# Moving block re-joins, a block sum, low parts and early weight sums from VectorE to GpSimd around two seven-product stages

## The chip, the cores and the metric

The kernel runs on one core of a Trainium2 chip. The core has a matrix engine (TensorE, PE in the profile), VectorE (DVE), ScalarE (ACT), GpSimd (POOL) and SyncE (SP, which here issues DMAs). Each engine works through its own list of instructions in order, and semaphores tie the lists together. The metric is the time of one execution in microseconds (us), the median over runs.

## The reference, cut to what matters

One transformer block over 1024 tokens of width 1024, with a context of 256 tokens. The part the change touches is two large projections in 32-bit floats:

```python
h_lat = _modulate(_rmsnorm(x, norm1_g), sh1, sc1)
u, v, q, k, vv, r, af, ab, ga, gb = split(h_lat @ w_in)     # w_in 1024 x 7200
b_lat = _gla_out(gated_linear_attention(q, k, vv, af, ab), r)   # 4 heads
a_lat = _chunk_mlp(u, v)
x = x + g1 * ((sigmoid(ga) * (a_lat @ w_branch_a) + sigmoid(gb) * (b_lat @ w_branch_b)) @ w_out)
h2 = _modulate(_rmsnorm(x, norm2_g), sh2, sc2)
a, g = split(h2 @ w_ffn_in)                                  # w_ffn_in 1024 x 5632
x = x + g2 * ((silu(g) * a) @ w_ffn_out)
return _rmsnorm(x, final_norm_g)
```

## The kernel before

A float32 product is made of three matrix passes: each operand is split into a high part (a rounded copy, made by ScalarE) and a low part (the operand less its high part, made by VectorE), and the passes are high by high, high by low and low by high. The split of a moving operand is `parts_of` (ScalarE L637, VectorE L638); that of a weight is `split_w` (ScalarE L236, VectorE L237).

The columns gb, u, r and ga of `w_in` (the "h stage", 16 column pairs in `todo`, 4 each) and all of `w_ffn_in` (the "FFN stage", 44 column blocks of 128 in 22 pairs) are multiplied by a scheme of seven block products instead of eight. The activations are four blocks B11, B12, B21, B22 (half of the 1024 inputs by 512 tokens) and the weights of a pair four blocks A11 to A22. The combinations are, for the activations, T3 = B22 − B12, T2 = T3 + B11, T1 = B12 − B11, T4 = B21 − T2, and for the weights S3 = A11 − A21, S2 = A22 − S3, S1 = S2 + A11, S4 = A12 − S2. The seven products are A11·B11, A12·B21, S3·T3, S2·T2, S1·T1, A22·T4 and S4·B22. One product is 12 matmuls of 128x512 (4 slices of the inputs by 3 passes). One pair is called a quad. The block raws and their parts are kept as two tiles of 128x1024 each, so that a combination of blocks is two vector instructions of 128x1024, and the low part two more. The weight sums S3, S2 (VectorE L700, L701) and S1, S4 (L702, L703) are four instructions of 128x512 per quad, followed by two low parts of 128x1024 (L638) and that of A22 (L710).

Ahead of a stage, when the activations' second half is not ready yet, the first quads do A11·B11 and A12·B21 alone (`early_quads`, six quads in the h stage, four in the FFN stage). `run_quads` then walks the pairs: for these early quads it does the other five products (`others`), for the later ones all seven. In `weights_s` the engine of S1 and S4 is an argument: GpSimd for the later quads, VectorE for the early ones.

`others` is the order around the change: S3·T3 into bank X, ScalarE copies X to q7 (L736), S2·T2 adds to X, VectorE makes u3 (L741), GpSimd q7 = u3 − q7 (L742), S1·T1 into bank Y, u3 += Y (L744), A22·T4 into X, p1 += X (L747), S4·B22 into Y, q7 += Y (L750). The five products of an early quad are 60 matmuls, a later quad's seven are 84.

The h stage sits behind the gated linear attention, a loop over four heads. A head's function calls `between`, which for heads 0 to 2 makes the gates of the next head, and for the last (head 3) emits four early quads of the h stage and `h_first`: B22 and B12 re-joined from their high and low parts (`h_raw`, L871), T3 = B22 − B12 in place (L877) and T3's parts. The rest of head 3 is scores (matmuls L565, masked copies L569, their sum att L573), outputs (matmuls L582, L583, L586), the norm's factor (rstd: VectorE L171, GpSimd L172, ScalarE L596), and a transpose back (PE L605, VectorE L610). After the loop come two more early quads and `h_others`: B11 re-joined, T1 over B12, T2 over B11, T1 and T2 split, B21 re-joined, T4 over B21. Early in head 3 the loop also makes two modulation vectors: VectorE multiplies and adds rows of `w_ada` (L930), PE spreads them (L934) and VectorE takes the diagonal (L936, L937).

In the FFN stage the blocks come raw from a transpose (`block_T`), and `other_operands` makes T3, T2, the first quad's weight sums (the callback `after`), T1, T4 and B22's parts, all combinations and low parts on VectorE.

The order on every engine but PE is set by a scheduler from the order in which the program is written and from when operands become ready; PE's order in these parts is that in which the matmuls are written. Tiles come from pools: 40 buffers of 128x1024 (`slot`), three raw weight tiles in flight, and eight banks of PSUM.

Of the kernel before, what the change touches and what calls it, by code (L numbers as in the profile page):

```python
# [17 lines left out]
P = 128  # L18
# [15 lines left out]
def block_kernel(  # L34
# [598 lines left out]

    def parts_of(raw, shape=(P, 2, 512)):

        hi, lo = slot(list(shape), F32R), slot(list(shape), F32R)
        nc.scalar.copy(hi, raw)  # L637
        nc.vector.tensor_sub(lo, raw, f(hi))  # L638
        return hi, lo
# [9 lines left out]

    def moving(tiles):  # L650
        return [parts_of(t) for t in tiles]

# [17 lines left out]
    def other_operands(op, blk, after):  # L670

        b11, b21, b12, b22 = blk[0][0], blk[1][0], blk[0][1], blk[1][1]
        dve = (nc.vector, nc.vector)
        t3 = combined("tensor_sub", b22, b12, dve)
        op["T3"] = moving(t3)
        t2 = combined("tensor_add", t3, b11, dve)
        op["T2"] = moving(t2)
        after()
        op["T1"] = moving(combined("tensor_sub", b12, b11, dve))
        op["T4"] = moving(combined("tensor_sub", b21, t2, dve))  # L680
        op["B22"] = moving(b22)

# [81 lines left out]
    def run_quads(op, todo, quads, hook=None):  # L764

        for fi, (w, cols, sink) in enumerate(todo):
            if fi < len(quads):
                if fi:
                    weights_s(*weights(w, cols), quads[fi]["ops"], nc.vector)
                others(quads[fi], op, sink)  # L770
# [95 lines left out]

    def h_raw(j, t):
        out = []
        for hi, lo in h_moving(j, t):
            o = slot([P, 2, 512])  # L870
            nc.vector.tensor_add(o, f(hi), f(lo))  # L871
            out.append(o)
        return out
# [10 lines left out]

    def h_others(op, b22, b12, after):
        b11 = h_raw(0, 0)
        in_place("tensor_sub", b12, b12, b11)
        in_place("tensor_add", b11, b11, b22)
        op["T2"] = moving(b11)
        after()  # L890
        op["T1"] = moving(b12)
        b21 = h_raw(1, 0)
        in_place("tensor_sub", b21, b21, b11)
        op["T4"] = moving(b21)
# [70 lines left out]
    for h in range(HEADS):  # L965
        now, ahead = ahead, None

        def between():
            if h + 1 < HEADS:
                global_next.append(head_gates(h + 1))  # L970
                return
            p1s.extend(four())
            for at in range(0, 4, 2):
                quads.extend(early_quads(h_op, todo, at, bank, p1s[at:at + 2]))
            sums.extend(h_first(h_op))
            global_next.append(None)
# [432 lines left out]
```

## Time and profile before

| | us |
|---|---|
| three runs | 1767.29, 1767.95, 1770.74 (median 1767.95) |
| profiled execution | 1771.97 |
| its span | 1770.2 |
| TensorE's mean granted clock in it | 0.993 of full speed |
| busy: PE, DVE, ACT, POOL | 1712.4 (97%), 1138.8 (64%), 668.5 (38%), 215.4 (12%) |

The busy rows say that PE is the engine that has work nearly always. The 3% in which it has none are spread over the span, and two slices of the profile's 40 are worse: PE shows 8 tenths at the start, and the clock row shows 8 tenths in slice 27 (1150 to 1195 us). The page gives each engine's mean over the whole span. What holds PE in a stretch is seen in the timeline of that stretch, where each row has a start, a time, the instruction with its count, and in brackets the idle time before it with the engine and tile whose event ended it.

### The profile page before, as it was taken

How to read it: one execution, taken by the hardware profiler on the slowest of the kernel's cores; microseconds unless marked ns; L12 is line 12 of the kernel's file. 1: busy time of each engine (PE TensorE's matmuls, PEld its weight loads, DVE VectorE, ACT ScalarE, POOL GpSimd, SP SyncE). 2: the span in 40 equal slices, each digit the busy share in tenths (PEclk: the TensorE clock that was granted, in tenths of full speed). 3: DMA queues.
4: the chain of work that ended last, by engine and by line, in shares of the span. 5: the costliest groups of instructions: out<-in, count | busy, mean ns of one | idle time of the engine just before them, and what ended most of it. 6: DMA issues, size and time to landing. Idle time of an engine off the chain costs nothing.

```text
span 1770.2 us, 21603 instructions
## 1 busy us (share of the span) xinstructions
PE 1712.4 (97%) x8162; PEld 1407.5 (80%) x8162; DVE 1138.8 (64%) x1559; ACT 668.5 (38%) x974; POOL 215.4 (12%) x193
## 2 busy tenths in 40 slices
PE   8899999999899999999999999989999999999997
PEld 3887888888678888877888888768888888888886
DVE  7686595867865464277656745885545555466797
ACT  6663423323443434234322213533333333355343
POOL 2220000000112353000000000012122122000001
PEclk9999999999999999999999999989999999999999
DMA  9511234052354454387858951233222232377572
GB/s 339 156 37 36 85 118 179 24 179 60 113 155 133 129 179 125 124 293 260 262 190 308 321 191 74 70 116 98 77 90 83 75 92 84 127 242 277 180 270 99
DMA packets 219961, 267.89 MB, mean 151 GB/s; under 512 B 11920, under 2 KB 142032, under 8 KB 219856
## 3 DMA queue, kind: packets, MB, share of 16 engines
q1 hardware_dynamic: 219040, 265.08, 45.1%
q0 software_dynamic: 720, 1.40, 0.2%
q8 instruction: 64, 1.05, 0.2%
q14 instruction: 41, 0.34, 0.1%
q10 hardware_dynamic: 96, 0.02, 0.0%
HBM read 205.64 MB, written 60.82 MB: 151 GB/s over the span
## 4 chain that ended last, share of the span: by engine, by line
PE 79%; DVE 11%; DMA 4%; issue 3%; ACT 3%; POOL 1%; SPq 0%; DVEq 0%; ACTq 0%; POOLq 0%
PE m L716 20%; PE g L716 17%; PE m L273 13%; PE m L1283 5%; PE g L1283 5%; PE m L1166 5%; PE m L285 4%; PE g L538 2%; DVE s L638 1%; PE m L822 1%; DVE wlo L237 1%; DVE s L422 1%; PE g L822 1%; DMA s<-in_w_ada_dram 1%; PE g L1363 1%
## 5 line engine op out<-in xcount | busy, mean ns | idle before, releaser
L716 PE MATMUL m<-s,s 128*128 128x512 f32 x1320 | 313.5, 395 | 8.8 <-ACT q L736 3.8
L716 PEld LDWEIGHTS m<-s,s 128*128 128x128 f32 x1320 | 251.0, 191 | 65.1 <-ACT q L736 5.8
L273 PE MATMUL m<-s,whi 128*128 128x512 f32 (+1 forms) x832 | 252.3, 384 | 2.2 <-ACT s L990 1.5
L237 DVE TENSOR_TENSOR wlo<-wr,whi 128x1024 fp32r<-128x1024 f32 x92 | 112.4, 1224 | 194.2 <-ACT whi L236 194.0
L716 PE MATMUL g<-s,s 128*128 128x512 f32 x960 | 225.0, 391 | 9.0 <-ACT q L736 4.1
L716 PEld LDWEIGHTS g<-s,s 128*128 128x128 f32 x960 | 179.2, 188 | 51.6 <-ACT q L736 6.6
L273 PEld LDWEIGHTS m<-s,whi 128*128 128x128 f32 x832 | 154.0, 188 | 33.2 <-ACT s L990 2.4
L236 ACT CAST whi<-wr 128x1024 fp32r<-128x1024 f32 x92 | 96.5, 1051 | 214.1 <-PE m L273 107.9
L273 PE MATMUL m<-s,wlo 128*128 128x512 f32 (+1 forms) x416 | 158.9, 383 | 1.8 <-DVE wlo L237 1.8
L637 ACT CAST s<-s 128x1024 fp32r<-128x1024 f32 x98 | 102.4, 1052 | 134.4 <-DVE s L638 62.2
L638 DVE TENSOR_TENSOR s<-s,s 128x1024 fp32r<-128x1024 f32 x98 | 145.4, 1494 | 9.9 <-ACT s L637 6.0
L172 POOL TENSOR_TENSOR rstd<-rstd,nhalf 128x1 f32<-128x1 f32 (+2 forms) x43 | 29.1, 678 | 847.7 <-DVE rstd L171 847.6
L285 PE MATMUL m<-whi,s 128*128 128x256 f32 x640 | 126.0, 291 | 0.1
L716 PE MATMUL g<-s,whi 128*128 128x512 f32 x384 | 118.5, 390 | 0.0
L638 DVE TENSOR_TENSOR s<-wr,s 128x1024 fp32r<-128x1024 f32 x77 | 92.3, 1233 | 22.8 <-ACT s L637 22.1
L285 PEld LDWEIGHTS m<-whi,s 128*128 128x128 f32 x640 | 101.5, 192 | 4.2 <-issue 2.7
L742 POOL TENSOR_TENSOR q<-u,q 128x512 f32<-128x512 f32 x38 | 59.4, 1563 | 314.1 <-DVE u L741 150.3
L637 ACT CAST s<-wr 128x1024 fp32r<-128x1024 f32 x77 | 78.2, 1053 | 49.9 <-DMA wr<-wsT 25.3
L285 PE MATMUL m<-wlo,s 128*128 128x256 f32 x320 | 92.3, 289 | 2.6 <-DVE wlo L237 1.9
L273 PEld LDWEIGHTS m<-s,wlo 128*128 128x128 f32 x416 | 78.3, 188 | 16.6 <-DVE wlo L237 2.0
L1166 PE MATMUL m<-s,s 128*128 128x512 f32 x384 | 87.6, 390 | 0.0
L1166 PEld LDWEIGHTS m<-s,s 128*128 128x128 f32 x384 | 72.0, 188 | 14.9
(293 smaller groups left out, 2879.2 us busy)
## 6 DMA issues: line engine op xcount, KB each, us to landing
wr<-in_w_in_dram SPq DMA_DIRECT2D x82, 512.0 KB
s<-in_w_ada_dram SPq DMA_DIRECT2D x48, 512.0 KB
wr<-in_w_ffn_in_dram SPq DMA_DIRECT2D x48, 512.0 KB
wr<-actd SPq DMA_DIRECT2D x77, 256.0 KB
s<-in_w_ffn_out_dram SPq DMA_DIRECT2D x22, 512.0 KB
wsT<-s SPq DMA_DIRECT2D x44, 256.0 KB
wr<-wsT SPq DMA_DIRECT2D x44, 256.0 KB
wr<-in_w_ffn_out_dram SPq DMA_DIRECT2D x33, 256.0 KB
```

The lines of the kernel that those rows point to most:

```text
L236: nc.scalar.copy(hi, raw)
L237: lo_sub[0] = nc.vector.tensor_sub(lo, raw, f(hi)).ins
L273: nc.tensor.matmul(ps, ws[a][:, k, :], get(b, k, t0, n), start=k == 0 and i == 0, stop=k == nk - 1 and i == 2)
L285: nc.tensor.matmul(ps[:, j, :], get(b, 4 * kh + k, (2 * tp + j) * P, P), ws[a][:, k, :], start=kh == 0 and j == 0 and k == 0 and i == 0, s ...
L538: r = nc.tensor.matmul(pkv[:, j, :], kt[:, j, :], vt(n), start=j == 0, stop=True, skip_group_check=True)
L637: nc.scalar.copy(hi, raw)
L638: nc.vector.tensor_sub(lo, raw, f(hi))
L716: pe(nc.tensor.matmul(ps, wts[a][:, k, :], mov[k // 2][b][:, k % 2, :], start=start and k == 0 and i == 0, stop=k == 3 and i == 2, skip_gr ...
L742: nc.gpsimd.tensor_sub(q7, u3, q7)
L822: pe(nc.tensor.matmul(banks[tt], op[mov][kp][b][:, kk, tt * P:(tt + 1) * P], wts[a][:, kk, :], start=start and kp == 0 and kk == 0 and i = ...
L1166: pe(nc.tensor.matmul(ps, yF.get(b, k, tt * P, P), wo[k // 2][a][:, k % 2, :], start=k == 0 and i == 0, stop=k == KT - 1 and i == 2))
L1283: pe(nc.tensor.matmul(banks[tt], o[b][:, 0, tt * P:(tt + 1) * P], o[a][:, 1, :], start=start and k == 0 and i == 0, stop=k == KH - 1 and i ...
```

## The change

In the h stage, B11 and B21 are re-joined on GpSimd (4 instructions of 128x1024) and the code that does it stands in `between` of the last head, ahead of the early quads, and no longer after the loop. T2 is made in place over T3's raw (B22's buffer) and T1 from B12 as before, T4 = B21 − T2.

In the FFN stage, T1 is computed on GpSimd right after T3, and the low parts of B22 are made on GpSimd ahead of `after`, where they stood last on VectorE.

In `run_quads`, S1 and S4 of the early quads but the first are added on GpSimd, which are five quads in the h stage and three in the FFN stage. The instruction counts are 1512 to 1488 on VectorE and 194 to 218 on GpSimd. ScalarE's and SyncE's do not change, and PE's list is the same, row by row. Below line 638 the line numbers are one higher than before, below 884 one lower.

```diff
-    def parts_of(raw, shape=(P, 2, 512)):
+    def parts_of(raw, shape=(P, 2, 512), eng=nc.vector):
...
-        nc.vector.tensor_sub(lo, raw, f(hi))
+        eng.tensor_sub(lo, raw, f(hi))
...
-    def moving(tiles):
-        return [parts_of(t) for t in tiles]
+    def moving(tiles, eng=nc.vector):
+        return [parts_of(t, eng=eng) for t in tiles]
...
-        dve = (nc.vector, nc.vector)
-        t3 = combined("tensor_sub", b22, b12, dve)
+        both = nc.vector, nc.vector
+        t3 = combined("tensor_sub", b22, b12, both)
+        t1 = combined("tensor_sub", b12, b11, (nc.gpsimd, nc.gpsimd))
         op["T3"] = moving(t3)
-        t2 = combined("tensor_add", t3, b11, dve)
+        t2 = combined("tensor_add", t3, b11, both)
         op["T2"] = moving(t2)
+        op["B22"] = moving(b22, nc.gpsimd)
         after()
-        op["T1"] = moving(combined("tensor_sub", b12, b11, dve))
-        op["T4"] = moving(combined("tensor_sub", b21, t2, dve))
-        op["B22"] = moving(b22)
+        op["T1"] = moving(t1)
+        op["T4"] = moving(combined("tensor_sub", b21, t2, both))
...
-                    weights_s(*weights(w, cols), quads[fi]["ops"], nc.vector)
+                    weights_s(*weights(w, cols), quads[fi]["ops"], nc.gpsimd)
...
-    def h_raw(j, t):
+    def h_raw(j, t, eng=nc.vector):
...
-            nc.vector.tensor_add(o, f(hi), f(lo))
+            eng.tensor_add(o, f(hi), f(lo))
...
-    def h_others(op, b22, b12, after):
-        b11 = h_raw(0, 0)
+    def h_others(op, b22, b12, b11, b21, after):
+        in_place("tensor_add", b22, b22, b11)
+        op["T2"] = moving(b22)
+        after()
         in_place("tensor_sub", b12, b12, b11)
-        in_place("tensor_add", b11, b11, b22)
-        op["T2"] = moving(b11)
-        after()
         op["T1"] = moving(b12)
-        b21 = h_raw(1, 0)
-        in_place("tensor_sub", b21, b21, b11)
+        in_place("tensor_sub", b21, b21, b22)
         op["T4"] = moving(b21)
...
+            raws = h_raw(0, 0, nc.gpsimd), h_raw(1, 0, nc.gpsimd)
             p1s.extend(four())
...
-            sums.extend(h_first(h_op))
+            sums.extend(h_first(h_op) + raws)
```

On VectorE in the tail of head 3, the rows before the change are the masked copies, the two sums att and the norm's factor (`rstd`, from the sums of squares `ss`), with the low part L638 of the h stage's T3 ahead of them:

```order
L638 TENSOR_TENSOR s_3964<-s_3951,s_3963 128x1024
L569 COPY_PREDICATED s_127<-mask_lo,g_3975 128x512
L573 TENSOR_TENSOR att_3981<-s_127 128x512
L569 COPY_PREDICATED s_127<-mask_up,g_3983 128x512
L569 COPY_PREDICATED s_127<-mask_lo,g_3989 128x512
L573 TENSOR_TENSOR att_3995<-s_127 128x512
L171 TENSOR_SCALAR rstd_4008<-ss_754_4005 128x2
L610 TENSOR_SCALAR s_3967<-g_4029,pcol 128x256
```

The same place after the change, where L878 is the in-place sum or difference (s_3957 and s_3959 are T2's tiles, s_3961 and s_3963 T1's, s_3819 and s_3821 the re-joined B11):

```order
L638 TENSOR_TENSOR s_3972<-s_3959,s_3971 128x1024
L569 COPY_PREDICATED s_127<-mask_lo,g_3983 128x512
L878 TENSOR_TENSOR s_3957<-s_3957,s_3819 128x1024
L573 TENSOR_TENSOR att_3989<-s_127 128x512
L878 TENSOR_TENSOR s_3959<-s_3959,s_3821 128x1024
L569 COPY_PREDICATED s_127<-mask_up,g_3991 128x512
L569 COPY_PREDICATED s_127<-mask_lo,g_3997 128x512
L878 TENSOR_TENSOR s_3961<-s_3961,s_3819 128x1024
L573 TENSOR_TENSOR att_4003<-s_127 128x512
L878 TENSOR_TENSOR s_3963<-s_3963,s_3821 128x1024
L171 TENSOR_SCALAR rstd_4016<-ss_758_4013 128x2
```

Four sums of 128x1024 have moved up from behind the head to between the masked copies and the factor.

On GpSimd, the rows of the same part after the change are the DMA of a row for the modulation, the four re-joins (L872), and the powers for the norm's factor (L172); before, the powers followed the DMA directly:

```order
L925 DMA s_3674<-in_b_ada_dram 1x16x64
L872 TENSOR_TENSOR s_3819<-s_921,s_925 128x1024
L872 TENSOR_TENSOR s_3821<-s_922,s_926 128x1024
L872 TENSOR_TENSOR s_3823<-s_923,s_927 128x1024
L872 TENSOR_TENSOR s_3825<-s_924,s_928 128x1024
L172 TENSOR_TENSOR rstd_4016<-rstd_4016,nhalf 128x2
```

The first of them takes a buffer that an ada row's product (L930 before, L929 after) held last.

On GpSimd at the start of the FFN stage after the change stand the norm's power, T1's two differences (L646), B22's two low parts (L638), the first quad's q7 (L743), and the weight sums of the second quad (L703, L704); before, q7 followed the norm's power directly:

```order
L172 TENSOR_TENSOR rstd_8958<-rstd_8958,nhalf 128x1
L646 TENSOR_TENSOR s_9183<-s_9037,s_8823 128x1024
L646 TENSOR_TENSOR s_9185<-s_9038,s_8824 128x1024
L638 TENSOR_TENSOR s_9208<-s_9039,s_9207 128x1024
L638 TENSOR_TENSOR s_9212<-s_9040,s_9211 128x1024
L743 TENSOR_TENSOR q_1595_9258<-u_1596_9259,q_1595_9258 128x512
L703 TENSOR_TENSOR s_9337<-s_9336,wr_9332 128x512
L704 TENSOR_TENSOR s_9337<-wr_9332,s_9336 128x512
```

Four instructions of 128x1024 are new ahead of the first q7, and two of 128x512 behind it.

## Rows read from the trace of the kernel before

**Rows 1.** Windows of 25 us: length, busy time of each engine (instructions), clock, DMA share, GB/s

```profile
450.00:475.00 25.00, 20.50 (x84) 15.15 (x83) 23.71 (x26) 13.21 (x15) 3.25 (x1) 1.00 0.23 63
1125.00:1150.00 25.00, 21.05 (x89) 16.11 (x88) 24.72 (x25) 13.57 (x15) 2.15 (x1) 1.00 0.28 83
1150.00:1175.00 25.00, 21.47 (x67) 16.49 (x68) 19.74 (x27) 9.58 (x13) 1.61 (x1) 0.73 0.36 107
```

**Rows 2.** Timeline of PE, h stage: start, us, instruction, [idle before <-releaser]

```profile
458.15 0.73 PE L716 MATMUL g<-s,s 128*128 128x512 f32 x2 [2.06 <-ACT s L637]
462.83 5.76 PE L716 MATMUL g<-s,s 128*128 128x512 f32 x24 [0.73 <-ACT q L736]
...
495.63 13.91 PE L716 MATMUL g<-s,s 128*128 128x512 f32 x60 [0.68 <-ACT q L736]
510.22 13.90 PE L716 MATMUL g<-s,s 128*128 128x512 f32 x60 [0.68 <-ACT q L736]
```

**Rows 3.** Timeline of PE, start of the FFN stage

```profile
1134.12 2.88 PE L716 MATMUL m<-s,s 128*128 128x512 f32 x12
1138.75 5.96 PE L716 MATMUL m<-s,s 128*128 128x512 f32 x25 [1.75 <-ACT q L736]
...
1150.16 5.04 PE L716 MATMUL m<-s,s 128*128 128x512 f32 x14 [1.55 <-DVE u L744]
1157.85 4.63 PE L716 MATMUL m<-s,s 128*128 128x512 f32 x10 [2.65 <-DVE s L638]
1163.20 15.87 PE L716 MATMUL m<-s,s 128*128 128x512 f32 x60 [0.72 <-ACT q L736]
1179.75 14.12 PE L716 MATMUL m<-s,s 128*128 128x512 f32 x60 [0.68 <-ACT q L736]
1194.55 5.74 PE L716 MATMUL m<-s,s 128*128 128x512 f32 x24 [0.68 <-ACT q L736]
```

**Rows 4.** Groups of POOL by form: line, op, shapes, count | busy, mean ns | idle before

```profile
L702 POOL TENSOR_TENSOR s<-s,wr 128x512 f32<-128x512 f32 x28 | 36.0, 1287 | 221.2 <-DVE s L701 146.9 <-PE g L716 30.7 <-issue 27.3
L196 POOL TENSOR_TENSOR s<-raw,s 128x256 fp32r<-128x256 f32 x4 | 3.1, 783 | 9.2 <-DVE raw L195 9.2
```

**Rows 5.** Timeline of DVE, head 3, early part

```profile
372.40 1.23 DVE L237 TENSOR_TENSOR wlo<-wr,whi 128x1024 fp32r<-128x1024 f32 x1 [0.18 <-ACT whi L236]
373.55 3.79 DVE L930 SCALAR_TENSOR_TENSOR s<-s,cs,s 128x1024 f32<-128x1024 f32 x3
...
393.23 1.29 DVE L483 SCALAR_TENSOR_TENSOR s<-m,s 128x512 f32<-128x512 f32 x2 [3.03 <-PE m L273]
394.44 1.28 DVE L936 TENSOR_TENSOR adat<-g,ident 128x512 f32<-128x512 f32 x2
```

**Rows 6.** Timeline of POOL, h stage

```profile
468.88 3.25 POOL L742 TENSOR_TENSOR q<-u,q 128x512 f32<-128x512 f32 x1 [24.93 <-DVE u L741]
499.91 1.60 POOL L742 TENSOR_TENSOR q<-u,q 128x512 f32<-128x512 f32 x1 [12.50 <-DVE u L741]
```

**Rows 7.** Timeline of DVE, beside those of POOL

```profile
468.62 2.35 DVE L638 TENSOR_TENSOR s<-s,s 128x1024 fp32r<-128x1024 f32 x2
...
500.40 1.66 DVE L702 TENSOR_TENSOR s<-s,wr 128x512 f32<-128x512 f32 x1
```

**Rows 8.** Timeline of DVE, head 3, tail

```profile
433.96 0.17 DVE L171 TENSOR_SCALAR rstd<-ss 128x2 f32<-128x2 f32 x1
...
448.72 4.62 DVE L877 TENSOR_TENSOR s<-s,s 128x1024 f32<-128x1024 f32 x4
```

**Rows 9.** Timeline of PE, head 3, tail

```profile
435.49 0.91 PE L605 MATMUL g<-ident,on 128*128 128x128 f32 x4
```

**Rows 10.** Timeline of DVE, start of the FFN stage

```profile
1132.96 2.43 DVE L638 TENSOR_TENSOR s<-s,s 128x1024 fp32r<-128x1024 f32 x2
```

**Rows 11.** Windows of 4 us of PE: length, busy (instructions), clock, DMA share, GB/s

```profile
36.00:40.00 4.00, 4.00 (x21) 0.50 1.03 411
56.00:60.00 4.00, 1.40 (x11) 1.00 0.02 4
```

## The prediction

> **What bounds the kernel now.** I read the page first: PE is busy for nearly the whole span, so a change on other engines is worth what it takes from PE's idle time, or from the time that PE runs at the lower of its two clock levels. Then windows of 25 us, to find where PE is idle [rows 1]: at the start of both stages that the change touches it works about 21 of 25 us, and there VectorE is busy 23.7 and 24.7 of 25, while GpSimd does 3.3 and 2.2. From 1150 us the mean granted clock is 0.73. So at these two places VectorE is the bound and GpSimd is free, and the question is what it takes to use that.
>
> The timeline of PE gives the sizes. In the h stage S3·T3 starts after 2.06 us of idle time [rows 2], on a ScalarE cast of VectorE's work. The five products of a quad take 13.9 us and a wait of 0.68 stands between two quads, so a quad that waits for nothing takes 510.22 − 495.63 = 14.59. From the first S2·T2 (462.83) to the third (495.63) are 32.80 us, two quads of 14.59 are 29.18: 3.6 us are lost. With the 2.06 ahead there are 5.7 to win. In the FFN stage from the first S2·T2 (1138.75) to the fourth (1194.55) are 55.80 us [rows 3], three quads are 43.77: 12.0 are lost. A part of that is clock: the 24 matmuls at 1150.16 and 1157.85 take 9.67 where 24 at 13.91/60 would be 5.56, so 4.1, and the quad at 1163.20 takes 15.87 for 13.91, so 1.96 more. Together a fall of the clock was worth 6.1 here, and 5.9 were waits.
>
> **The h stage.** Four costs and gains.
>
> The re-joins on GpSimd. No row of 128x1024 on GpSimd exists. 128x512 is 1.29 us and 128x256 is 0.78 [rows 4], so 0.51 per 256 columns, and 128x1024 about 1.29 + 2 × 0.51 = 2.3; I call it an estimate. They start when the first ada products free their buffers, near 372 us, and so run beside the chain of VectorE's multiply-adds [rows 5]. Does one engine hold up the other? The trace has it both ways: GpSimd's q7 at 499.91 ran to 501.51, and VectorE's L702 issued at 500.40 took 1.66 where it otherwise takes 0.69, ending 0.55 after it; but GpSimd's q7 at 468.88, issued just after two low parts of VectorE, took 3.25, and VectorE's two took 2.35 as ever [rows 6, 7]. The one issued second waits. All of these are two-tensor operations; no row has the multiply-add beside GpSimd. If it is held like them: four spells of 2.3 less the 0.14 that overlap (0.69 − 0.55), so 2.2 each, 8.8 us; VectorE was idle 0.18 and 3.03 in this stretch [rows 5], which takes 3.2 off, and the diagonal at 394.44, for which PE waits with its next banks, is late by 5.6. If it isn't held: 0. Between them I take two thirds, 3.7, since four instructions queued back to back on each side will alternate, and VectorE is then the second more often than not. Both ends stay for the range.
>
> The Trainium skill's page "SBUF — State Buffer", section "Who interferes with whom", says that "A DVE instruction with two SBUF inputs contends with a GpSimd instruction that reads SBUF", and that issue order decides which one blocks. The two meetings above agree with it (1.66 for 0.69). By the rule the multiply-add, which has two tensor inputs, would be held too, this term would be 5.6 and my sum 1.9 higher; no row here shows that form.
>
> The sums in the tail. In the built order four sums of 128x1024 stand between the masked copies and the norm's factor of head 3. Behind that factor on VectorE are queued the other factors and the scalings L610; for it wait GpSimd's power, ScalarE's scaling, and PE's transpose at 435.49, which had no time to spare [rows 9]. A sum is 4.62 / 4 = 1.16 us [rows 8], four are 4.6; about 0.3 of it falls in VectorE's gaps between these copies, so the factor goes from 433.96 to 438.3 and PE is late by 4.3. I see no way in which this costs nothing: the order is fixed and the sums have all their inputs by then. If the re-joins are late themselves, it is more.
>
> What is won behind it. From VectorE at the start of the stage go the four re-joins and the two thirds of the in-place work that have now been done, 6 × 1.16 = 6.9 us behind 445, four of them the 4.62 [rows 8]. T2's low parts are then ready when the early quads end, the 2.06 goes, and the T1 and T4 work, which held the first two quads, is ahead of PE. I count the whole of the loss as won: early quads ended at 458.15 − 2.06 = 456.1 [rows 2] and now end at 456.1 + 3.7 + 4.3 = 464.1, S3·T3 takes 2.8, the wait 0.68, so S2·T2 starts at 467.6, the third one 29.18 later at 496.7. Before it was 495.63 [rows 2]: +1.1.
>
> The weight sums of five early quads on GpSimd take 2 × 1.29 us instead of 2 × 0.69 each. A quad is 14.59 us and the low parts of the sums are wanted only near its end for the next one, so I count nothing; were that cover gone, it would be 1.2 a quad, and a held VectorE up to 1.2 more, as in the row at 500.40. This goes for the FFN's three quads as well.
>
> So the h stage gives +1.1, with +3.0 and −2.6 as its ends (5.6 and 0 for the 3.7).
>
> **The FFN stage.** T1's two differences and B22's two low parts go to GpSimd, 4 × 1.16 = 4.6 us off VectorE, and q1's sums another 1.4. But they are early: T1 runs beside T3's split, B22's low parts beside the first quad's weight sums, with VectorE full [rows 1]. What these four hold VectorE up is again between 0 and 4 × 2.2 = 8.8; two thirds are 5.9. For S3's low part PE waits: it came at 1132.96 + 1.2 = 1134.1, and S3·T3 started at once [rows 3, 10]. So S3·T3 moves to 1134.1 + 5.9 = 1140.0, S2·T2 to 1140.0 + 2.9 + 0.68 = 1143.6, 4.8 later than now. From there VectorE has only T1's split and T4 before A22·T4, six instructions of 1.16 with the sums' second low part and A22's (1.2 and 0.7), 8.9 us for the 9 that PE needs until then; the quads run free, and the fourth S2·T2 stands at 1143.6 + 43.77 = 1187.4, where it was 1194.55: −7.2. That keeps the clock up throughout. If nothing is held, all 12.0 are won.
>
> **The clock.** The idle time is now in two larger pieces: in the tail of head 3 PE has a wait of over 4 us, and from the early quads' end, near 1135, to 1140 nearly nothing. Did such pieces lower the clock before? Both answers are in the rows: from 1150 to 1175, where the 24 matmuls stand between waits, the mean is 0.73 [rows 1, 3], and at 36 us a busy PE has 0.50; yet at 56 to 60 us, with PE busy 1.40 of 4, it is 1.00 [rows 11]. I take one short fall at each place, at the price of the quad at 1163.20, 1.96 each: 3.9.
>
> **Sum.** 1.1 − 7.2 + 3.9 = −2.2 on 1771.97 for the profiled execution: 1769.8. This execution was 4.0 above the median of the runs, 1767.95, and the change is taken off that: 1765.7.
>
> **The rivals.**
>
> *Clearly faster.* GpSimd is the one that gives way, as at 468.88 [rows 6], or the clock doesn't fall. With the 3.7 and 5.9 held but no fall it is 1.1 − 7.2 = −6.1, 1761.8; with nothing held and no fall −2.6 − 12.0 = −14.6, 1753.3. The middle is 1757. For it: four of GpSimd's instructions are issued in the open, and one can begin only behind VectorE's running one. Against: VectorE's list is full there, so that it meets all of them.
>
> *Slower.* Place: the two idle pieces above. Mechanism: the fall of the clock is whole, as it was at 1150, not short. Price: 6.1 each instead of 1.96, −6.1 + 12.2 = +6.1: 1774.0. It decides where PE does less than it did between 1147 and 1160 before, when the clock fell. For it: 1137 to 1140 would have no matmul at all. Against: the 1.00 at 56 to 60.
>
> *No effect on either.* What the h stage loses in the tail it wins at the quads, and in the FFN stage PE waits for something that doesn't move (raw weights from DMA, three tiles in flight, or ScalarE's casts, whose B22 parts now stand ahead of S3's): 1768, within a few tenths per cent.
>
> **How the numbers follow.** About 3.5 us, 0.2%, is what a measurement of this kernel can tell from no change. My forecast 0.40; clearly faster 0.27; slower 0.21; no effect 0.12. The forecast's own range is 1761 to 1770, a fall more or fewer on either side, and lies partly below 1764.4: of its 0.40 I count 0.14 as faster, 0.22 as the same, 0.04 as slower. Of no effect 0.10 is the same and 0.02 slower. That gives faster 0.41, same 0.32, slower 0.27. For 8 in 10 the range goes to the middle of the faster rival, a little beyond, and to the slower one with 1.9 for the re-joins: 1755 to 1776.
>
> **What would show it.** Re-joins: rows L929 on VectorE between 372 and 390 of 2.5 us or more instead of 1.26 (3.79 / 3), and L935 near 398 to 400; if they stay at 1.26 and GpSimd's four take over 3 us each, the faster rival has it. Tail: L171 on VectorE over 4 us after the second att, and PE's first L605 with an idle time of about 4. h stage: S2·T2 60 matmuls in one piece from the first quad on. FFN: S3·T3 starting on a VectorE low part near 1140 plus what the h stage shifts, and the next three S2·T2 at distances of 14.6. Clock: windows of 3 us behind both pieces, at 1.00 or near 0.5. I would be wrong if PE's waits of the first FFN quads stay where they are, or if PE's clock is low for more than 10 us behind either piece.

## The result and the profile after

The changed kernel takes 1790.04 us (median of 4, 1788.08 to 1791.47) against 1767.62 for the kernel before on the same chip: ratio 1.0124, 95% interval 1.0108 to 1.014, so 22.4 us slower. The profiled execution took 1790.48, its span is 1788.7. VectorE's busy time fell from 1138.8 to 1131.6, GpSimd's rose from 215.4 to 265.2, and PE's waits grew at the two places that the change was made for. The two spans differ by 18.5 and the medians by 22.4: the execution of the kernel before that was profiled stood 4.0 above the median of its runs.

Windows of 25 us of the kernel after, with the columns of [rows 1]; the FFN stage has moved on by 13 us:

```profile
425.00:450.00 25.00, 18.99 (x93) 15.93 (x93) 19.02 (x23) 7.24 (x16) 3.43 (x2) 0.86 0.17 43
475.00:500.00 25.00, 20.84 (x89) 16.30 (x89) 15.13 (x19) 8.96 (x13) 10.23 (x7) 1.00 0.48 137
1150.00:1175.00 25.00, 21.10 (x72) 15.62 (x71) 19.43 (x20) 11.20 (x13) 6.50 (x4) 0.80 0.17 47
1175.00:1200.00 25.00, 18.22 (x71) 14.27 (x72) 16.80 (x22) 8.40 (x11) 8.59 (x6) 0.93 0.51 154
```

VectorE, the third busy figure, is no longer full in these rows, 15 to 19 of 25 (from 1125 to 1150, where the FFN stage's operands are made, it still does 22.07), and PE does no better: 18.22 of 25 in the last row, where the kernel before had 23.65. VectorE's load alone doesn't explain that; the timelines below show what PE waits for.

PE's list is the same in both kernels, so the n-th matmul of one trace can be set against the n-th of the other (8162 in each). PE is late by 3.2 us after the re-joins (at 407 us of before), by 4.2 at att (432), by 9.3 at the norm's factor (436), by 12.8 after two clock falls (447); it is back at 9.6 at the first S2·T2, at 10.6 at the second, at 10.4 in the third and fourth quad and at 13.9 in the sixth. The FFN stage begins 13.0 late and ends 18.1 late.

Early part of head 3, VectorE's multiply-adds and GpSimd's re-joins (answers to [rows 5]):

```profile
373.70 7.95 DVE L929 SCALAR_TENSOR_TENSOR s<-s,cs,s 128x1024 f32<-128x1024 f32 x3
...
382.78 6.88 DVE L929 SCALAR_TENSOR_TENSOR s<-s,cs,s 128x1024 f32<-128x1024 f32 x3
```

```profile
372.74 3.30 POOL L872 TENSOR_TENSOR s<-s,s 128x1024 f32<-128x1024 f32 x1 [8.16 <-DVE s L929]
377.20 10.05 POOL L872 TENSOR_TENSOR s<-s,s 128x1024 f32<-128x1024 f32 x3 [1.16 <-DMA s<-in_w_ada_dram]
```

Three multiply-adds took 3.79 and 3.92 before and take 7.95 and 6.88 beside GpSimd. Each engine holds the other, as single rows from the same place show:

```profile
378.36 3.30 DVE L929 SCALAR_TENSOR_TENSOR s<-s,cs,s 128x1024 f32<-128x1024 f32 x1
```

```profile
377.20 3.37 POOL L872 TENSOR_TENSOR s<-s,s 128x1024 f32<-128x1024 f32 x1 [1.16 <-DMA s<-in_w_ada_dram]
380.53 3.39 POOL L872 TENSOR_TENSOR s<-s,s 128x1024 f32<-128x1024 f32 x1
```

The first of these two GpSimd sums ends at 380.57, the multiply-add issued beside it 1.1 later (381.66), and the GpSimd sum issued beside that one 2.3 later again (383.92).

Tail of head 3 on VectorE, GpSimd and PE (answers to [rows 8, 9]):

```profile
440.03 1.22 DVE L878 TENSOR_TENSOR s<-s,s 128x1024 f32<-128x1024 f32 x1
441.16 0.23 DVE L171 TENSOR_SCALAR rstd<-ss 128x2 f32<-128x2 f32 x2
441.30 2.35 DVE L878 TENSOR_TENSOR s<-s,s 128x1024 f32<-128x1024 f32 x2
```

```profile
441.47 2.76 POOL L172 TENSOR_TENSOR rstd<-rstd,nhalf 128x2 f32<-128x2 f32 x1 [54.22 <-DVE rstd L171]
```

```profile
444.79 1.27 PE L605 MATMUL g<-ident,on 128*128 128x128 f32 x4 [5.00 <-ACT on L596]
```

L171 comes late, behind four sums, as forecast. But right behind it VectorE issues T4's two sums, and GpSimd's first power, 0.69 to 0.71 otherwise, takes 2.76 beside them. PE waits 5.00 where before it started at once [rows 9], and does nothing from 441 to 444.

PE in the FFN stage (answers to [rows 3]):

```profile
1153.16 4.63 PE L717 MATMUL m<-s,s 128*128 128x512 f32 x10 [2.69 <-DVE s L638]
1158.46 16.00 PE L717 MATMUL m<-s,s 128*128 128x512 f32 x60 [0.68 <-ACT q L737]
1176.68 8.46 PE L717 MATMUL m<-s,s 128*128 128x512 f32 x36 [2.21 <-ACT q L737]
1186.12 5.73 PE L717 MATMUL m<-s,s 128*128 128x512 f32 x24 [0.99 <-DVE u L745]
1195.97 10.07 PE L717 MATMUL m<-s,s 128*128 128x512 f32 x36 [4.12 <-ACT q L737]
```

The waits of 2.21 and 4.12 on ScalarE's copy of q7 are new. ScalarE's own rows at the second of them, with what it waited for in brackets:

```profile
1188.82 1.06 ACT L637 CAST s<-s 128x1024 fp32r<-128x1024 f32 x1 [2.09 <-DVE s L702]
1192.41 1.04 ACT L637 CAST s<-s 128x1024 fp32r<-128x1024 f32 x1 [2.53 <-POOL s L704]
1193.36 0.62 ACT L1255 ACTIVATE p<-p 128x512 f32<-128x512 f32 x1
1193.89 1.03 ACT L236 CAST whi<-wr 128x1024 fp32r<-128x1024 f32 x1
1194.83 0.61 ACT L710 CAST s<-wr 128x512 fp32r<-128x512 f32 x1
1195.35 0.57 ACT L737 COPY q<-m 128x512 f32<-128x512 f32 x1
```

S3·T3 ended at 1186.12 + 5.73 = 1191.85, and the copy was made at 1195.35: it stood behind the cast of S1 and S4, which waited for GpSimd's sum, and behind what was queued after that cast. At the first, 2.21, the way is over VectorE: the copy waited for an instruction (L1259) that stood behind the low part of S1 and S4.

The wait of the fifth early quad of the h stage looks alike on PE, and is another one. PE, and then ScalarE:

```profile
537.12 15.79 PE L717 MATMUL g<-s,s 128*128 128x512 f32 x60 [2.62 <-ACT q L737]
```

```profile
535.45 0.62 ACT L710 CAST s<-wr 128x512 fp32r<-128x512 f32 x1 [2.53 <-DMA gbd<-s]
...
536.50 0.56 ACT L737 COPY q<-g 128x512 f32<-128x512 f32 x1
```

Here the cast of A22 ahead of the copy waited for a store to end (`gbd<-s`, which frees a shared buffer), and not for a sum. In the kernel before this cast did not wait.

### The profile page after: what moved, and what is told of

Its sections match the earlier page's. It is cut to its first block, busy times and chain, and to the rows that moved or that the text cites. A ratio compares the mean times of both kernels' runs of the same rounds, so it can differ in the third digit from the quotient of the medians.

```text
span 1788.7 us, 21636 instructions
## 1 busy us (share of the span) xinstructions
PE 1718.0 (96%) x8162; PEld 1412.5 (79%) x8162; DVE 1131.6 (63%) x1535; ACT 667.7 (37%) x974; POOL 265.2 (15%) x217
## 5 line engine op out<-in xcount | busy, mean ns | idle before, releaser
L717 PEld LDWEIGHTS m<-s,s 128*128 128x128 f32 x1320 | 250.9, 191 | 68.9 <-ACT q L737 9.7
L236 ACT CAST whi<-wr 128x1024 fp32r<-128x1024 f32 x92 | 96.4, 1051 | 214.0 <-PE m L273 106.2
L638 DVE TENSOR_TENSOR s<-s,s 128x1024 fp32r<-128x1024 f32 x96 | 144.6, 1516 | 29.5 <-ACT s L637 16.8
L172 POOL TENSOR_TENSOR rstd<-rstd,nhalf 128x1 f32<-128x1 f32 (+2 forms) x43 | 31.2, 725 | 833.7 <-DVE rstd L171 833.7
L638 DVE TENSOR_TENSOR s<-wr,s 128x1024 fp32r<-128x1024 f32 x77 | 92.3, 1233 | 23.4 <-ACT s L637 22.7
L743 POOL TENSOR_TENSOR q<-u,q 128x512 f32<-128x512 f32 x38 | 56.5, 1487 | 234.5 <-ACT s L637 118.0
L703 POOL TENSOR_TENSOR s<-s,wr 128x512 f32<-128x512 f32 x36 | 46.4, 1289 | 261.0 <-DVE s L702 139.6
```

The lines of the kernel that those rows point to most:

```text
L172: nc.gpsimd.tensor_tensor(r[:, :n], r[:, :n], nhalf[:, :n], op=ALU.pow)
L638: eng.tensor_sub(lo, raw, f(hi))
L703: eng.tensor_add(s14[:, 0], s32[:, 1], a11)
L717: pe(nc.tensor.matmul(ps, wts[a][:, k, :], mov[k // 2][b][:, k % 2, :], start=start and k == 0 and i == 0, stop=k == 3 and i == 2, skip_gr ...
L743: nc.gpsimd.tensor_sub(q7, u3, q7)
```

## The experiments

Times are medians; "before" is the kernel before, run on the same chip (1767.4 to 1768.2 over the calls), with the ratio's 95% interval. An order edge is a dependency that carries no data and only fixes which of two instructions comes first in an engine's list; in the cuts of code below the calls that add one are shortened, and "..." stands for lines left out.

**Undoing one part of the changed kernel at a time.** The sums of the early quads back on VectorE:

```diff
-                    weights_s(*weights(w, cols), quads[fi]["ops"], nc.gpsimd)
+                    weights_s(*weights(w, cols), quads[fi]["ops"], nc.vector)
```

> The changed kernel (1790.0 us) with the weight sums of the early quads back on VectorE, nothing else. Theory Q (ScalarE's queue): the low part of S1 and S4 is cast by ScalarE only when GpSimd has made the sums, and ScalarE's copy of q7 is queued behind that cast, so S2T2 waits for it. Then the waits of 2.62 us (fifth quad of the h stage), 2.21 and 4.12 (second and third of the FFN stage) fall back to 0.68, which is 6.9, and the two short clock falls right behind them go, some 1.6 each: about 10 us faster than the changed kernel, 1780. Rival D: these waits come from raw weights that land late, or from the shift of the rest, and the sums are hidden as the prediction had it: 1788 to 1791.

1775.92, ratio 1.0042 (1.0029 to 1.0055): 14.1 faster than the changed kernel. The waits ahead of S2·T2 in the h stage's early quads are 0.68 to 0.74 again. That is more than the 10 at which the waits and falls were put: the edit is the largest part of the loss.

The h stage back (in `h_others` and `between`):

```diff
+        b11 = h_raw(0, 0)
...
+        b21 = h_raw(1, 0)
...
-            raws = h_raw(0, 0, nc.gpsimd), h_raw(1, 0, nc.gpsimd)
...
-            sums.extend(h_first(h_op) + raws)
+            sums.extend(h_first(h_op))
```

> The changed kernel with the h stage's re-joins and in-place sums as they were before (VectorE, behind the heads), the FFN operands and the early weight sums as changed. Theory Q: the h stage's part lost about 10 us up to the second quad's S2T2 (PE is late by 10.6 there), so about 10 faster, 1780. Rival P (the prediction's sum): the part costs 1.1 plus one short clock fall, so 1787 to 1789.

1781.72, ratio 1.0078 (1.0064 to 1.0092): 8.3 faster. Nearer to theory Q.

The FFN operands back (`other_operands` as before):

```diff
-        t1 = combined("tensor_sub", b12, b11, (nc.gpsimd, nc.gpsimd))
...
-        op["B22"] = moving(b22, nc.gpsimd)
         after()
-        op["T1"] = moving(t1)
...
+        op["T1"] = moving(combined("tensor_sub", b12, b11, dve))
...
+        op["B22"] = moving(b22)
```

> The changed kernel with the FFN operands as they were before (T1's differences and B22's low parts on VectorE, in the old order), the rest as changed. PE's lateness goes from 13.0 at the FFN stage's start to 11.5 in the second quad in the changed kernel. Theory Q: the operands alone are worth some 1.5 us, or a little more since the sums' waits hide a part: 1790 to 1794. Rival P (the prediction's sum): they are worth 7.2, and only the sums' waits covered it: 1797. Rival C: they cost, by the later first S3T3 and the clock: 1785 to 1788.

1784.84, ratio 1.0095 (1.0081 to 1.0109): 5.2 faster, at the edge of rival C. The part costs; both other theories fall.

The in-place sums behind the head:

```diff
-            getattr(nc.vector, op)(d, a, b)
+            ins = getattr(nc.vector, op)(d, a, b)
+            add_manual_dep(ins, last_scaling)   # order only
```

> The changed kernel with one order edge added: the in-place sums T2, T1, T4 of the h stage stand on VectorE behind the last scaling of head 3 instead of among its masked copies; the re-joins stay on GpSimd. Theory T (tail): the 1.2 us at att and the 5.1 at the norm's factor go, and with them the two clock falls (1.9 and 1.6); a part, up to the 5.7 that the kernel before lost there, is paid again behind the head: 4 to 8 faster than the changed kernel, 1782 to 1786. Rival R (the re-joins alone): the lateness comes from the re-joins beside the multiply-adds, and the tail only passes it on: 1789 to 1791.

1781.2, ratio 1.0077 (1.0064 to 1.0091): 8.8 faster, a little over theory T. One edge gives as much as undoing the whole part: the tail, not the re-joins, is what the h stage lost. In this kernel's trace PE is still 3.1 later behind the re-joins (0.9 late at 350 us of before, 4.0 at 407), nothing is added in the tail (4.05 at 447), and 2.1 of it is won back by the second quad.

**One part alone on the kernel before.** The early sums on GpSimd:

```diff
-                    weights_s(*weights(w, cols), quads[fi]["ops"], nc.vector)
+                    weights_s(*weights(w, cols), quads[fi]["ops"], nc.gpsimd)
```

> The kernel before with one edit of the change: S1 and S4 of the early quads added on GpSimd. Theory Q (ScalarE's queue) with the 14.1 us that the changed kernel gained when this edit was undone: most of it is there alone, 8 to 14 slower than before, 1776 to 1782, with waits of 2 us and more on ScalarE's q7 copy in quads after the first of both stages. Rival X (the edits cost only together, since VectorE and PE are at other places then): within 3 us of before.

1779.59, ratio 1.0066 (1.0054 to 1.0078): 11.6 slower. The price is that foreseen, the waits are not: on q7 only one is over 2 us (2.78, in the fifth quad of the h stage, again behind a cast of A22 that waits 2.69 for a store), and on u3 there are new ones of 2.83 in the h stage and of 1.95 and 1.94 in the FFN stage. In the second FFN quad of this kernel PE waits for u3; PE, VectorE and GpSimd:

```profile
1175.97 5.73 PE L716 MATMUL m<-s,s 128*128 128x512 f32 x24 [1.95 <-DVE u L744]
```

```profile
1171.82 1.23 DVE L638 TENSOR_TENSOR s<-s,s 128x1024 fp32r<-128x1024 f32 x1 [1.67 <-ACT s L637]
1172.96 0.69 DVE L710 TENSOR_TENSOR s<-wr,s 128x512 fp32r<-128x512 f32 x1
1174.63 0.69 DVE L700 TENSOR_TENSOR s<-wr,wr 128x512 f32<-128x512 f32 x1 [0.98 <-DMA wr<-in_w_ffn_in_dram]
1175.24 0.68 DVE L744 TENSOR_TENSOR u<-m,u 128x512 f32<-128x512 f32 x1
```

```profile
1167.17 1.29 POOL L702 TENSOR_TENSOR s<-s,wr 128x512 f32<-128x512 f32 x1 [6.01 <-issue]
1168.41 2.28 POOL L703 TENSOR_TENSOR s<-wr,s 128x512 f32<-128x512 f32 x1
```

GpSimd needs 3.5 us for the two sums, the second held; the low part (L638) waits 1.67 for their cast, the next quad's first sum 0.98 for a raw weight, and u3, whose operands were there, comes behind both. S4·B22, which writes the bank that u3 reads, waits for it.

The FFN operands alone (the same edit as in the third run, the other way):

> The kernel before with the FFN operands of the change alone (T1's differences and B22's low parts early and on GpSimd). The changed kernel was 5.2 faster without this edit. Theory C (clock and lock): B22's low parts hold VectorE at S1 and S2's sums, S3T3 starts some 5 late and PE stands still long enough for the clock to fall in every run; what is won behind it does not pay for that: 1769 to 1773. Rival P (the prediction's term): 1760 to 1764. Rival X (the cost was only there beside the late sums): 1766 to 1768.

1770.54, ratio 1.0012 (1.0004 to 1.0021): 2.5 slower, theory C. PE in this kernel, and its windows of 3 us (busy, clock):

```profile
1139.96 4.63 PE L717 MATMUL m<-s,s 128*128 128x512 f32 x10 [2.70 <-DVE s L638]
1145.27 13.55 PE L717 MATMUL m<-s,s 128*128 128x512 f32 x50 [0.68 <-ACT q L737]
...
1162.82 13.89 PE L717 MATMUL m<-s,s 128*128 128x512 f32 x60 [1.06 <-ACT q L737]
```

```profile
1138.00:1141.00 3.00, 1.04 (x3) 0.64 0.29 82
1141.00:1144.00 3.00, 3.00 (x9) 0.50 0.62 180
1144.00:1147.00 3.00, 2.33 (x6) 0.50 0.29 88
1147.00:1150.00 3.00, 3.00 (x10) 0.65 0.00 0
```

Beside B22's low parts VectorE's L702 and L703 took 2.77 and 2.73 us instead of 0.69 each; ten matmuls of S3·T3 then stand 2.70 later, and at half clock.

The h stage's part alone:

> The kernel before with the h stage's part of the change alone (re-joins of B11 and B21 on GpSimd early in head 3, T2 over T3, in-place sums where the order puts them). Undone in the changed kernel it gave back 8.3. If parts add: 6 to 10 slower than before, 1774 to 1778, with PE late by 3 after the re-joins, by 5 more at the norm's factor, and 2 of it won back in the first two quads. If it costs less alone (fewer waits behind it): 1769 to 1772.

1774.12, ratio 1.0032 (1.0019 to 1.0044): 5.9 slower, at the lower edge of its first forecast. With 11.6 and 2.5 the three parts alone make 20.0 of the 22.4.

**Two parts mended.**

> The changed kernel with two of its parts mended: the early weight sums on VectorE, and the in-place sums T2, T1, T4 behind the last scaling of head 3. If the parts add: 1790.0 − 14.1 − 8.8 = 1767.1; what is left against before is the re-joins (3 late, some of it won back in the first two quads) and the FFN operands: 1764 to 1769. If the gains overlap, since less idle time is there to be taken: 1770 to 1773.

1769.79, ratio 1.0007 (0.9998 to 1.0016). Between the two forecasts, and not told from before.

**How the sums cost.** ScalarE's list: the cast of S1 and S4 behind the copy.

```diff
-        nc.scalar.copy(q7, X)
+        copied = nc.scalar.copy(q7, X)
+        split(s14, ("S1", "S4"), after=copied)   # an early quad's; order edge on the cast
```

> The changed kernel with GpSimd's sums kept, but ScalarE's cast of S1 and S4 of an early quad (and so VectorE's low part) put behind that quad's copy of q7 instead of ahead of it. Theory Q: the q7 copy no longer waits for GpSimd, the waits of 2 to 4 us at S2T2 fall to 0.7; S1T1 may then wait a little for the low part, 1 us a quad; so 6 to 10 faster than the changed kernel, 1780 to 1784. Rival B (blocking of VectorE by GpSimd, or raw weights held longer): the order on ScalarE doesn't matter, 1788 to 1791.

1788.26, ratio 1.011 (1.0095 to 1.0126): 1.8 faster than the changed kernel, which its spread (1785.03 to 1790.55) doesn't set apart from it, so theory Q as put there falls. The waits of 2.2 to 4.1 on q7 are gone, but each early quad now waits 0.7 to 1.0 for u3, and PE loses 3.8 more at the first later quad (late by 14.9 at 548 us of before, by 18.8 at 564, where the changed kernel stays at 13.9).

Raw tiles: four in flight, on the changed kernel and on the one before.

```diff
-tile_pool(name="slots", bufs=40), tile_pool(name="wraw", bufs=3)
+tile_pool(name="slots", bufs=39), tile_pool(name="wraw", bufs=4)
```

> The changed kernel with four raw weight tiles in flight instead of three (and 39 shared buffers instead of 40), nothing else. Theory D (held raw weights): GpSimd's second sum is the last reader of a raw tile, the next load is issued when it ends (488.11 us right behind a sum that ended at 488.09, in the kernel with the sums edit alone), and VectorE's next weight sum waits for its landing with u3 queued behind it; with one tile more the load is ahead: 5 to 9 faster than the changed kernel, 1781 to 1785. Rival W (the wait is for the sums themselves: 3.5 us on GpSimd instead of 1.4, with ScalarE's cast, VectorE's low part and GpSimd's q7 queued behind them): within 2 of 1790.

> The kernel before with four raw weight tiles in flight and 39 shared buffers: the control of the run above, and a version that might win. VectorE waits 0.92 and 1.20 us for raw weights in single quads there, at places where other waits lie behind: 1765 to 1768, so no more than 3 of what the run above gains is common to both.

1797.84 (1.0166, 1.0152 to 1.018), 7.8 slower than the changed kernel, and 1769.05 (1.0004, 0.9995 to 1.0013). Theory D falls, and rival W, which had 1790, is missed too. What is seen is ScalarE's list once more: in the fourth and fifth quads of the h stage PE waits 3.98 and 4.01 for q7's copy, which stands behind a cast of a later quad's weight (L236) that waited 2.77 and 2.81 for its load. Why the order comes out so isn't settled: in the h stage a low part also waited 2.10 for a store to free its buffer, and this kernel has one shared buffer less while four hold the re-joined blocks. So the run doesn't say what held raw weights cost.

VectorE's list, and then both lists:

```diff
-        nc.vector.tensor_sub(s32[:, 0], a11, a21)
+        first = nc.vector.tensor_sub(s32[:, 0], a11, a21)
+        add_manual_dep(first, u3_done)   # the quad before's second u3 sum; order only
```

> The kernel before with the early sums on GpSimd (1779.6 by itself, 11.6 slower than before), and one order edge more: on VectorE the next quad's first weight sum stands behind this quad's second u3 sum instead of ahead of it. Theory V (VectorE's order): with the sums on GpSimd, VectorE stands at the next quad's first weight sum, which waits for a raw weight that GpSimd still holds, and u3, for which PE waits (1.94 three times in the FFN stage, 2.83 and 0.75 in the h stage), is queued behind it; with the edge these waits go: 5 to 8 faster, 1771.5 to 1775. Rival A (ScalarE's order: q7's copy behind the cast): the waits move to the q7 copy, 1778 to 1781.

> As the run above, and on ScalarE the cast of S1 and S4 stands behind the quad's q7 copy too, so that neither list has a wait on GpSimd's sums ahead of what PE waits for. If both lists together are the cost: within 3 of before, 1767 to 1771. If it is the length of the way itself (3.5 us of sums on GpSimd instead of 1.4, then cast, low part, S1T1): no better than with one of the edges, 1775 to 1780.

1782.65 (1.0075, 1.0063 to 1.0088) and 1782.54 (1.0087, 1.0074 to 1.0101): no better than the sums alone, and beyond all four ranges. With one edge the waits went to the other list, 1.76 on q7 in three quads. With both, the trace shows more than the median does. PE in the h stage of the second:

```profile
480.64 13.89 PE L728 MATMUL g<-s,s 128*128 128x512 f32 x60 [0.83 <-ACT q L748]
...
524.36 13.90 PE L728 MATMUL g<-s,s 128*128 128x512 f32 x60 [0.68 <-ACT q L748]
...
562.04 1.22 PE L728 MATMUL m<-s,whi 128*128 128x512 f32 x2 [4.61 <-ACT p L738]
```

The second to fifth early quads run free, with the sums on GpSimd, and PE is 0.7 ahead of before at the sixth (539.7). The price comes behind it: 1.2 late at 548, within the sixth quad, and 8.6 at 564, in the first later quad, whose copy of p1 stands behind a cast that waits for GpSimd. So the edge on the cast was put on the later quads too:

> The kernel before with the early sums on GpSimd and both order edges (u3 ahead of the next quad's first weight sum on VectorE, q7's copy ahead of the cast of S1 and S4 on ScalarE), the second edge now for the later quads too. With the edges on the early quads alone these ran at 14.57 us each and PE was level with before (+0.33) up to the sixth quad; then a wait of 4.61 came at the first later quad, whose copy of p1 stands behind such a cast. Theory L (the in-order lists are the whole cost): with that copy free too, most of the 6 to 8 lost there goes: 1769 to 1775. Rival W (raw tiles are released later by the longer sums, so that the first later quad's weights land late whatever the order): 1779 to 1783.

1787.21 (1.0111, 1.0097 to 1.0124), the slowest of these and beyond both ranges. Its trace says more: at 564 us PE is late by 0.9, of which 0.5 is from ahead of the stage, so with both lists free the early sums cost 0.4 up to the first later quad, where the sums without the edges cost 7.6 (0.6 late ahead of the stage, 8.2 at 564). In the later quads, with the second edge on them, PE falls back: by 700 us it is 10.5 late, with waits of 1.5 for u3 in several quads; the kernel with that edge on the early quads alone loses nothing there (8.6 at 564 and at 700). So the order of the lists is shown as what the sums cost up to there. Two ends stay open: the edges also took away the wait for a store in the fifth quad, behind which 3.5 of the 7.6 stand (4.7 late in the fourth quad, 8.2 in the sixth), and the runs don't tell buffers from order in that part; and no order tried made the sums on GpSimd free over the whole kernel.

**Versions that might win.** The re-joins left on VectorE, one behind each pair of scalings of head 3's tail:

```diff
+                if gap:
+                    gap(jp - 1)     # h_raw of one tile on VectorE, behind the last scaling
```

> The kernel before with the re-joins of B11 and B21 kept on VectorE, but one put behind each pair of scalings in the tail of head 3, where VectorE was idle about 2.1 us three times (439.47, 442.50, 445.66 in the trace of before); the order puts in-place sums beside them. Theory T (VectorE's place in the order, not its load, is what the h stage lacked): up to 4.6 us leave the busy stretch behind the head, of the 5.7 lost there 3 to 5 are won: 1763 to 1765. Rival: the factor L171 is held again by two sums a gap, and it is the same or slower: 1768 to 1771.

1765.52, ratio 0.9984 (0.9975 to 0.9992): 2.7 faster than before, less than the 3 to 5 expected; the trace has 1.9 of it in the h stage. VectorE in this kernel (L894 the re-join, L881 an in-place sum, L612 a scaling):

```profile
437.43 1.22 DVE L894 TENSOR_TENSOR s<-s,s 128x1024 f32<-128x1024 f32 x1
438.68 1.23 DVE L881 TENSOR_TENSOR s<-s,s 128x1024 f32<-128x1024 f32 x1
439.82 0.48 DVE L612 TENSOR_SCALAR s<-g,pcol 128x256 f32<-128x256 f32 x1
```

The gap of 2.08 before 439.47 of before is filled, and the scaling is 0.35 later.

With the u3 edge on it, and T1 alone of the FFN part, on before and on this version:

> The version with the re-joins in the gaps of head 3's tail (1765.5), all sums on VectorE, with the same order edge (next quad's first weight sum behind this quad's second u3 sum). In the kernel before, PE waits 0.36 and 1.55 for u3: if VectorE's order costs there too, 1 to 2 faster, 1763.5 to 1764.5; if the sums come later by the edge and S3T3 waits: 1766 to 1769.

> The kernel before with T1's two differences of the FFN stage on GpSimd and early, B22's low parts left on VectorE. The FFN part as a whole (with B22's low parts on GpSimd, early) is 2.5 slower than before. Theory: B22's low parts are the harm, since they hold VectorE's two weight sums (2.77 and 2.73 us instead of 0.69 each) for which S3T3 waits; T1 holds T3's two differences only 1.9 in sum and takes 2.35 off later: 1765.5 to 1768. Rival: T1 is as bad: 1769 to 1771.

> The version with the re-joins in the gaps of head 3's tail (1765.5 where before was 1768.2), with T1's differences of the FFN stage on GpSimd too. If T1 alone is worth 0 to 2, 1763.5 to 1766; if it costs, 1766 to 1769.

1766.38 (0.9993, 0.9984 to 1.0001), 1765.78 (0.9993, 0.9984 to 1.0002) and 1765.28 (0.9984, 0.9975 to 0.9993). The edge gives nothing. T1 alone can't be told from before; with B22's low parts on GpSimd and early as well it was 2.5 slower, so the FFN part's loss is with these. The best two versions, 1765.5 and 1765.3, are one time.

## Why the prediction was wrong

The forecast was 1765.7 with a range to 1776, and 0.27 for slower. 1790.0 lies beyond the range. Alone, the three parts measured 5.9 (h stage), 2.5 (FFN stage) and 11.6 (early sums), where 1.1, −7.2 and 0 were forecast and 3.9 for the clock. Point by point:

**The early sums, the step that failed.** The prediction says "I count nothing", since "the low parts of the sums are wanted only near its end for the next one". They cost 11.6 alone and 14.1 beside the rest. The slack was there for the sums' own reader and not for what is queued behind them: the cast waits on ScalarE with q7's copy behind it, the low part waits on VectorE with u3 behind it, and PE waits for both. The cover that was named, a quad of 14.59 us, hides an instruction only if nothing urgent stands behind its waiting readers. With both lists free the cost was 0.4 up to the first later quad. The prediction's own price for a lost cover, 1.2 to 2.4 a quad, is 9.6 to 19.2 for eight quads; it was named and left out of the sum and the range. In the fifth quad of the h stage the list stood for a store and not for a sum, so that way of losing time is a third one, seen in the trace and not tested by itself.

**The re-joins, right in size, in part by luck.** Forecast 3.7 between 0 and 5.6; PE was late by 3.2. The open question, whether the multiply-add is held too, is answered: six took 7.95 and 6.88 instead of 3.79 and 3.92. The 3.7 was a weight between held and not held, and it is the held end that came true: the diagonal came 4.0 later (398.41 for 394.44), since VectorE lost 7.1, not 8.8, and its idle time took about as much of it as forecast. The estimate of 2.3 for a GpSimd sum was good: it ran 3.3 to 3.4, but it ends 2.3 after the multiply-add that held it. That GpSimd is held in its turn was in [rows 6, 7] and not in the sum.

**The tail, the mechanism right and the size short.** Forecast 4.3; 9.3 − 3.2 = 6.1. L171 came 4.0 later than the re-joins account for (441.16 for 433.96, less 3.2). The other 2.1 are GpSimd's power, held by T4's sums, which the built order puts right behind L171 (2.76 instead of 0.7). Winning back behind it was forecast at 8.0 − 1.1 = 6.9; with the early sums on VectorE it was 6.6 (12.96 late at 447, 6.35 from the fourth quad on), in the changed kernel 2.4 (12.8 to 10.4): the sums' waits took the rest.

**The FFN stage, wrong in sign.** Forecast −7.2, measured +2.5 alone. The hold was right: 5.9 forecast; in the changed kernel T3's two differences took 1.74 and 2.52 instead of 1.23 each (1.8), the two weight sums 2.77 and 2.73 instead of 0.69 each (4.1). Three things were not. With the FFN operands alone the clock was down from 1138 to 1150 (windows above), not for a short time, and S2·T2 began at 1145.27, where 1143.6 was forecast. The quads behind did not run free: waits of 1.06 on q7 and 2.27 on u3 were left. And the 12.0 us to be won were read from one execution with a clock fall worth 6.1, itself 4.0 above the median of its runs. In the kernel with the h stage's part alone, whose FFN stage is as before, the first S2·T2 and the fourth are these:

```profile
1141.56 5.97 PE L716 MATMUL m<-s,s 128*128 128x512 f32 x25 [1.75 <-ACT q L736]
...
1193.34 6.87 PE L716 MATMUL m<-s,s 128*128 128x512 f32 x29 [0.68 <-ACT q L736]
```

That is 51.78 instead of 55.80, so 8.0 were lost there and not 12.0 (8.1 in the version with the re-joins in the gaps, whose FFN stage is as before too). With the FFN operands alone it is 49.28: 2.5 of the 8.0 were won, for a first S2·T2 that came 6.5 later.

**The clock.** Two short falls, 3.9 in all, were forecast. In the two stages of the changed kernel there were five, windows of 3 us of PE (busy, clock):

```profile
441.00:444.00 3.00, 0.00 (x0) 0.72 0.00 0
444.00:447.00 3.00, 2.21 (x7) 0.50 0.02 5
456.00:459.00 3.00, 3.00 (x10) 0.50 0.04 14
538.00:541.00 3.00, 3.00 (x9) 0.50 0.95 274
1159.00:1162.00 3.00, 3.00 (x8) 0.50 0.00 0
1197.00:1200.00 3.00, 3.00 (x9) 0.50 0.65 186
```

By the timelines they cost some 11.5: 3.5 for the first two (PE goes from 9.3 to 12.8 late), 1.9 in the quad of 15.79 at 537.12, 4.4 at the start of the FFN stage (10 matmuls in 4.63 and 60 in 16.00, where 2.32 and 13.90 are usual) and 1.7 at 1195.97 (36 in 10.07 instead of 8.34). The falls at 538 and 1197 stand behind the waits of 2.62 and 4.12 on q7 that came with the early sums. The row that spoke against a fall, a PE busy 1.40 of 4 at full clock [rows 11], was one execution's luck. Up to there PE's list is the same in all kernels of this case, and the window behind it reads so, in the kernel before and in the changed one:

```profile
60.00:64.00 4.00, 4.00 (x34) 1.00 0.53 142
60.00:64.00 4.00, 4.00 (x23) 0.57 0.64 151
```

In all the other traces of this case the clock falls there too.

**The rivals.** The slower one had the right mechanism for a part and was priced at 1774. None was about the lists behind the sums, the largest cost.

## What to carry to other kernels

When an instruction moves to a slower engine, follow its reader: on each engine where a reader will wait, look at what is queued behind it, and price that. An instruction that GpSimd takes from a full VectorE isn't gone: where both read two operands from SBUF, VectorE stood still for most of the time that GpSimd ran (two weight sums of 0.69 took 2.77 and 2.73, so 4.1 were lost beside 5.4 us of GpSimd). And a row of one execution, such as a clock that did not fall, is weak evidence until a second execution shows it. It paid better to leave the work on VectorE and move it into gaps between instructions that wait for PE.

## What the runs showed of the hardware

That the hold goes both ways stood in [rows 6, 7]. Not expected: it reaches very small instructions. GpSimd's power on 128x2 took 2.76 us beside two VectorE sums, instead of 0.7. A GpSimd sum of 128x1024 took 3.3 to 3.4 us beside multiply-adds and 2.7 to 2.9 on average beside two-tensor instructions; counted from the end of the multiply-add that held it, it is 2.3.

The Trainium skill's "SBUF — State Buffer", section "Who interferes with whom", says that a VectorE instruction with two SBUF inputs contends with a GpSimd instruction that reads SBUF, and that issue order decides which one blocks. The trace agrees with the first for the multiply-add too, which no row of before had shown: 2.65 and 2.29 on average instead of 1.26. It agrees with the second at the re-joins, where the one issued second waits, in turn. It does not at the tail: the power, issued at 441.47, is ahead of the second of T4's two sums, yet both sums take their usual 1.2 (2.35 for two, to 443.65) and the power ends 0.6 behind them. The row of q7 at 468.88, read in the prediction as issued behind two low parts, is the same case: the two began at 468.62 and took 2.35 as ever.
